# A hybrid conformer / gated-DeltaNet trunk layer on one Trainium2 core: the engine queues ordered by another scheduler simulation

## The chip, the cores and the metric

The kernel runs on one core of one Trainium2 chip, as one program with one launch. The metric is device time in microseconds (us), from three executions of each kernel; the median is what counts. A profile of one more execution gives a trace: every instruction of the five engines with its start and duration, the DMA packets and the semaphore events. TensorE (PE) does the matmuls and weight loads (PEld), VectorE (DVE) and ScalarE (ACT) do elementwise work, GpSimd (POOL) a little of it, SyncE (SP) issues nearly all the DMAs. Each engine works through a queue of its own, in the order in which the program was built; an instruction whose semaphore is not there yet holds up everything behind it on that engine.

## The reference

One layer, for 256 prompt positions and 64 sample positions together (T = 320 columns), D = 2048:

```python
h = rmsnorm(x, g_pre_mix)
p = h @ w_in                                   # 6160 columns
a_out = conformer_conv(p[..., :2048], ...)     # GLU, depthwise conv of 31 taps, group norm, silu
b_out = gdn_mixer(p[..., 2048:], ...)          # conv of 4 taps, silu, l2norm, chunked delta rule, gated norm
x = x + rmsnorm(jnp.concatenate([a_out, b_out], axis=-1) @ w_out, g_post_mix)
h = rmsnorm(x, g_pre_ffn)
gu = causal_dwconv(h @ w_up, ffn_buf, w_ffn_dw, b_ffn_dw)   # 2 x 5632 columns, 3 taps
gate, up = jnp.split(gu, 2, axis=-1)
x = x + rmsnorm((jax.nn.silu(gate) * up) @ w_down, g_post_ffn)
```

Besides both outputs, all four recurrent states are returned for both groups of positions.

## The kernel before, in words

Everything lies transposed: 128 channels on the partitions, the 320 positions along the free axis. A product of float32 accuracy is made from rounded operands: a weight tile `w` is split into `whi` (ACT, the cast of line 217) and `wlo = w - whi` (DVE, line 218), an activation likewise into `hi` and `lo`, and three matmuls of 128x128 by 320 columns replace one (weights `whi` by `hi`, `whi` by `lo`, `wlo` by `hi`; lines 233, 234 and 237 in `block_matmul`). So each 512 KB of weights costs a DMA by SP (line 210 in `load_dma`), a cast by ACT, a subtraction by DVE and 24 matmuls. The pools `wst` (raw weights) and `wsp` (split weights) have three buffers each: SP's next weight load waits for a DVE subtraction, ACT's next cast waits for matmuls.

The stages, in order:

- **Start** (lines 285 to 405): x, its scale vectors and the weights of four column blocks (`w_first`, in pairs of k: line 324) are loaded, scaled and split, and PE works through four blocks at once (`ps_first`, lines 398 and 400).
- **Input projection with both mixers** (to line 1003): 48 column blocks. The mixers' own steps are generators that are advanced between the dense matmuls. Among them are the gates (`psg`, line 479), and, for each head, squares, scales and copies on ACT (`vh`, `kd`, `kds`; lines 689 to 711).
- **Output projection** (`psm`, to line 1078): in two parts; the second (lines 1067 to 1069, five k of the sixteen) also loads x again in 16 pieces (line 1056) and two tiles of `w_up` ahead of time, all through SP's queue.
- **The middle norm** (lines 1082 to 1105): the row sums end in `rstd` (`pst`, line 259) and `rstd_rows` (`psb`, line 272), with matmuls on zeros between them (`keep_warm`, `psw`, line 280). Then, for each of the 16 k: `m[k]` times the norm (DVE, line 1099), the residual sum (DVE, line 1100), the cast to `hi2[k]` (ACT, line 1104) and `lo2[k]` (DVE, line 1105). The weights of the next stage are split in between (lines 1090 to 1095).
- **First group of the up-projection** (`up_group`, lines 1114 to 1124): four column blocks at once, so that PE can begin with k = 0 while the later k are still being made: 12 matmuls for each k, of which the first eight read `hi2[k]` and the last four `lo2[k]`.
- **ConvFFN** (to line 1207): the other 84 column blocks of `w_up`, with conv and gate on DVE and ACT, and, four times, 16 blocks of `w_down` (`psdn`). The row sums of the new x are made with `square_acc` (line 1040) and used after the first blocks (`second_norm`).
- **End**: the last norm, residual by matmul (`fin`) and the output.

The order of each queue is not written out. The program is traced in the order of the code; every instruction gets a priority (its place, shifted by `high_priority`), `issue_after` adds an order between two instructions of one engine, and the tile framework's scheduler then plays the program through in a simulation of its own, takes at each step the instruction of best priority among those it holds to be ready, and writes the queues down in the order in which it took them. The lines on which most below rests:

```python
            with ExitStack() as e:
                if 0 < k < 4:
                    e.enter_context(tc.issue_after(added))
                V.tensor_tensor(m[k], m[k], rb1, ALU.mult)
            added = V.tensor_tensor(x1[:, k, :], x1[:, k, :], m[k], ALU.add).ins
...
            S.activation(hi2[k], x1[:, k, :], AF.Identity, scale=g)
            split = V.scalar_tensor_tensor(lo2[k], x1[:, k, :], g, hi2[k].bitcast(F32), ALU.mult, ALU.subtract).ins
...
            for n, (wt, x) in enumerate(((hi, xh), (lo, xh), (hi, xl))):
                for i in range(4):
                    o = i * 256 + k % 2 * P
                    PE.matmul(pss[i][:, 0:T], wt[:, o:o + P], x, start=(k == 0 and n == 0), stop=(k == KB - 1 and n == 2))
```

## Time and profile before

| what | us |
|---|---|
| three executions | 1485.42, 1484.97, 1485.43 (median 1485.42) |
| the profiled execution | 1485.64 |
| its span, first to last instruction | 1483.9 |
| PE busy, PEld busy | 1474.3, 1452.9 |
| DVE, ACT, POOL busy | 994.5, 734.1, 234.0 |
| bytes moved by DMA | 224.22 MB, 151 GB/s on the mean |

Times in the trace count from the first instruction. A row of the timeline has start, duration, engine, line, operation and tiles; several alike in a row are merged (xcount), and the idle time of the engine before a row stands in brackets with what ended it. Matmuls overlap each other in the records: each lasts about 0.31 us, yet one starts every 0.147 us. So a wait of PE shows in the distance of two starts, and the brackets give less than the whole of it.

### The profile page before, as it was taken

What the parts mean: (1) busy time and instruction counts of PE and PEld (TensorE: products, weight loads), DVE (VectorE), ACT (ScalarE), POOL (GpSimd) and SP (SyncE); (2) the same over time, 40 slices, a digit from 0 to 9 for tenths busy, and PEclk for the clock granted to TensorE, in tenths of its full rate; (3) what the DMA queues carried; (4) which work ended last, traced back from release to release, by engine and by line L of the source; (5) the groups of instructions that cost most, each with busy time, mean ns of one, the idle gap of its engine ahead of it and who ended that gap; (6) DMA issues with size and microseconds to landing.
All of it is one profiled execution on the core that took longest, in us unless ns stands there. A gap on an engine that the chain in (4) does not pass through costs nothing.

```text
span 1483.9 us, 27312 instructions
## 1 busy us (share of the span) xinstructions
PE 1474.3 (99%) x10626; PEld 1452.9 (98%) x10626; DVE 994.5 (67%) x1812; ACT 734.1 (49%) x1355; POOL 234.0 (16%) x390
## 2 busy tenths in 40 slices
PE   9999999999999999999999999999999999999998
PEld 8999999999999989999999999999999999999997
DVE  6779888889998778765336666445666445666554
ACT  7774656665554746544334444334444334444453
POOL 0111101121010001332002222002322001223101
PEclk9999999999999999999999999999999999999999
DMA  8435453545444734444554444554444445444453
GB/s 287 148 115 157 159 162 113 151 155 147 123 126 144 243 122 142 156 143 132 147 176 144 155 148 130 146 161 164 148 150 140 137 149 173 148 156 142 137 148 119
DMA packets 98281, 224.22 MB, mean 151 GB/s; under 512 B 18792, under 2 KB 39528, under 8 KB 98152
## 3 DMA queue, kind: packets, MB, share of 16 engines
q1 hardware_dynamic: 98008, 222.45, 47.4%
q8 instruction: 83, 1.36, 0.4%
q14 instruction: 46, 0.38, 0.1%
q10 hardware_dynamic: 144, 0.03, 0.0%
HBM read 215.33 MB, written 7.12 MB: 150 GB/s over the span
## 4 chain that ended last, share of the span: by engine, by line
PE 94%; ACT 2%; DVE 1%; DMA 1%; issue 1%; POOL 0%; SPq 0%; ACTq 0%; DVEq 0%
PE psu L237 13%; PE psu L234 13%; PE psu L233 13%; PE psdn L233 7%; PE psdn L234 7%; PE psdn L237 7%; PE psq L233 3%; PE psq L234 3%; PE psq L237 3%; PE psm L233 2%; PE psm L234 2%; PE psm L237 2%; PE psu L1123 1%; PE psv L233 1%; PE psgate L233 1%; PE psgate L237 1%
## 5 line engine op out<-in xcount | busy, mean ns | idle before, releaser
L217 ACT CAST whi<-w 128x1024 fp32r<-128x1024 f32 (+2 forms) x440 | 413.1, 941 | 484.6 <-PE psu L234 169.6
L218 DVE TENSOR_TENSOR wlo<-w,whi 128x1024 fp32r<-128x1024 f32 (+2 forms) x440 | 477.1, 1085 | 194.6 <-ACT whi L217 126.6
L234 PE MATMUL psu<-lo,whi 128*128 128x320 f32 x1344 | 397.0, 309 | 0.0
L233 PE MATMUL psu<-hi,whi 128*128 128x320 f32 x1344 | 396.9, 309 | 0.0
L234 PEld LDWEIGHTS psu<-lo,whi 128*128 128x128 f32 x1344 | 252.3, 188 | 0.0
L233 PEld LDWEIGHTS psu<-hi,whi 128*128 128x128 f32 x1344 | 252.3, 188 | 0.0
L237 PE MATMUL psu<-hi,wlo 128*128 128x320 f32 x1344 | 224.3, 309 | 0.0
L237 PEld LDWEIGHTS psu<-hi,wlo 128*128 128x128 f32 x1344 | 204.0, 188 | 0.0
L234 PE MATMUL psdn<-gl,whi 128*128 128x320 f32 x660 | 195.9, 310 | 0.0
L1156 POOL COPY nffn<-fbuf 128x2 f32<-128x2 f32 x88 | 101.6, 1155 | 587.2 <-DVE fbuf L1154 584.0
L1154 DVE TENSOR_TENSOR fbuf<-psu,rb 128x256 f32<-128x256 f32 x88 | 37.4, 424 | 168.7 <-PE psu L237 168.7
L233 PE MATMUL psdn<-gh,whi 128*128 128x320 f32 x480 | 142.8, 309 | 0.0
L234 PEld LDWEIGHTS psdn<-gl,whi 128*128 128x128 f32 x660 | 123.9, 188 | 0.3
L233 PE MATMUL psq<-hh,whi 128*128 128x320 f32 x352 | 105.9, 314 | 0.0
L234 PE MATMUL psq<-hl,whi 128*128 128x320 f32 x352 | 104.1, 309 | 0.0
L233 PEld LDWEIGHTS psdn<-gh,whi 128*128 128x128 f32 x480 | 90.1, 188 | 0.0
L237 PE MATMUL psdn<-gh,wlo 128*128 128x320 f32 x480 | 89.8, 309 | 0.0
L237 PEld LDWEIGHTS psdn<-gh,wlo 128*128 128x128 f32 x480 | 75.3, 188 | 0.0
L233 PEld LDWEIGHTS psq<-hh,whi 128*128 128x128 f32 x352 | 66.1, 188 | 0.5 <-issue 0.2
L234 PEld LDWEIGHTS psq<-hl,whi 128*128 128x128 f32 x352 | 66.1, 188 | 0.2
L563 DVE SCALAR_TENSOR_TENSOR cvt<-ub,par,cvt 128x320 f32<-128x320 f32 x120 | 65.2, 544 | 0.1
L1199 DVE TENSOR_TENSOR y<-y,psdn 128x320 f32<-128x320 f32 x45 | 22.0, 488 | 59.1 <-PE psdn L237 59.1
(356 smaller groups left out, 2477.1 us busy)
## 6 DMA issues: line engine op xcount, KB each, us to landing
w<-in_w_up SPq DMA_DIRECT2D x176, 512.0 KB
w<-in_w_in SPq DMA_DIRECT2D x88, 512.0 KB
w<-in_w_down SPq DMA_DIRECT2D x64, 384.0 KB
w<-in_w_down SPq DMA_DIRECT2D x64, 320.0 KB
w<-in_w_out SPq DMA_DIRECT2D x32, 320.0 KB
w<-in_w_out SPq DMA_DIRECT2D x16, 384.0 KB
w<-in_w_first SPq DMA_DIRECT2D x6, 512.0 KB
wtp<-wsp SPq DMA_DIRECT2D x4, 640.0 KB
```

Of the source, the lines that this page charges most:

```text
L217: S.copy(hi[:, 0:width], w[:, 0:width])
L218: V.tensor_tensor(lo[:, 0:width], w[:, 0:width], hi[:, 0:width].bitcast(F32), ALU.subtract)
L233: tick(PE.matmul(ps, wh, xh, start=(first and k0 + j == 0), stop=False))
L234: tick(PE.matmul(ps, wh, xl, start=False, stop=False))
L237: tick(PE.matmul(ps, lo[:, j * P:(j + 1) * P], xh, start=False, stop=(final and k0 + j == nk - 1)))
L563: return lambda: V.scalar_tensor_tensor(acc, x, w, acc, ALU.mult, ALU.add)
L1123: PE.matmul(pss[i][:, 0:T], wt[:, o:o + P], x, start=(k == 0 and n == 0), stop=(k == KB - 1 and n == 2))
L1154: V.tensor_tensor(buf[:, 2:258], psu[:, 0:TP], rb2[:, 0:TP], ALU.mult)
L1156: G.tensor_copy(nffn[:, b, 0, :], buf[:, 256:258])
L1199: V.tensor_tensor(y[:, n, :], y[:, n, :], psd[:, 0:T], ALU.add)
```

## The change

The tile framework has a second simulation that its scheduler can play the program through. It follows the engines and transfers more finely than the default. One argument selects it:

```diff
-    with tile.TileContext(nc) as tc:
+    with tile.TileContext(nc, schedule_with_timeline_sim=True) as tc:
         trunk_kernel(tc, ins, outs)
```

No operation, tile, buffer or priority changes; what changes is the order in each engine's queue, and with it the places of some waits. (Two loads of activation tables on ACT fall away, since functions of one table now stand together more often.) PE's order is nearly the old one; the mixers' small matmuls stand some matmuls earlier or later among the dense ones. Three places where DVE, SP and ACT differ:

DVE in the middle norm, before. Here `m` with a number is `m[k]`: 5575, 5658, 5714 and 5766 are k = 2, 3, 4 and 5, `psb` is the norm's row, `lo_0` to `lo_3` are `lo2[0]` to `lo2[3]`, and `wlo` is a split of the weights for the first group:

```order
L1105 SCALAR_TENSOR_TENSOR lo_0_6880<-x_6336,par,hi_0_6879 128x320
L218 TENSOR_TENSOR wlo<-w,whi 128x1024
L1105 SCALAR_TENSOR_TENSOR lo_1_6892<-x_6336,par,hi_1_6891 128x320
L1100 TENSOR_TENSOR x_6336<-x_6336,m_5575 128x320
L1099 TENSOR_TENSOR m_5658<-m_5658,psb 128x320
L1099 TENSOR_TENSOR m_5714<-m_5714,psb 128x320
L1105 SCALAR_TENSOR_TENSOR lo_2_6898<-x_6336,par,hi_2_6897 128x320
L1100 TENSOR_TENSOR x_6336<-x_6336,m_5658 128x320
L218 TENSOR_TENSOR wlo<-w,whi 128x1024
L1105 SCALAR_TENSOR_TENSOR lo_3_6910<-x_6336,par,hi_3_6909 128x320
L1100 TENSOR_TENSOR x_6336<-x_6336,m_5714 128x320
L1099 TENSOR_TENSOR m_5766<-m_5766,psb 128x320
```

The same place now; 6842 is k = 15, and the marks stand for one more multiplication and `lo_1`, with nine multiplications behind it, and for ten sums:

```order
L1105 SCALAR_TENSOR_TENSOR lo_0_6880<-x_6336,par,hi_0_6879 128x320
L218 TENSOR_TENSOR wlo<-w,whi 128x1024
L1100 TENSOR_TENSOR x_6336<-x_6336,m_5575 128x320
L1099 TENSOR_TENSOR m_5658<-m_5658,psb 128x320
L1099 TENSOR_TENSOR m_5714<-m_5714,psb 128x320
...
L1099 TENSOR_TENSOR m_6842<-m_6842,psb 128x320
L1105 SCALAR_TENSOR_TENSOR lo_2_6898<-x_6336,par,hi_2_6897 128x320
L1100 TENSOR_TENSOR x_6336<-x_6336,m_5658 128x320
L218 TENSOR_TENSOR wlo<-w,whi 128x1024
L1100 TENSOR_TENSOR x_6336<-x_6336,m_5714 128x320
...
L1100 TENSOR_TENSOR x_6336<-x_6336,m_6842 128x320
L1105 SCALAR_TENSOR_TENSOR lo_3_6910<-x_6336,par,hi_3_6909 128x320
```

Before, DVE went k by k; now all multiplications (line 1099) stand ahead of `lo_2`, and all sums (line 1100) ahead of `lo_3`. Ahead of `lo_1` stand one sum and three multiplications more than before, between `lo_1` and `lo_2` ten multiplications (k = 6 to 15), between `lo_2` and `lo_3` thirteen sums and one split.

SP in the second part of the output projection, before; `w<-in_w_out` is a weight load of that part, `x` a piece of x, `w<-in_w_up` a tile for the first group of the up-projection:

```order
L210 DMA w<-in_w_up 128x4x256
L1056 DMA x_6336<-in_x 128x320 x5
L210 DMA w<-in_w_out 128x640
L1056 DMA x_6336<-in_x 128x320 x2
L210 DMA w<-in_w_out 128x640 x2
L1056 DMA x_6336<-in_x 128x320
```

And now:

```order
L210 DMA w<-in_w_up 128x4x256
L1056 DMA x_6336<-in_x 128x320 x8
L210 DMA w<-in_w_out 128x640
L1056 DMA x_6336<-in_x 128x320
L210 DMA w<-in_w_out 128x640
```

Three pieces of x more stand ahead of the first weight load; further on, one piece of x and `fpar` (line 1058) now follow the second `w_up` tile at once, where a weight load stood.

ACT among the steps of a head in the input projection, before; `whi` is a cast of dense weights, the other rows are the head's own scales (`vh`, `kds`) and silu (`kq`):

```order
L710 ACTIVATE kds_599<-tv_1296,sc 64x128
L711 ACTIVATE vh<-tv_1296,sc 128x128
L636 ACTIVATE kq<-cq 128x256
L637 ACTIVATE kqs<-cq 128x64
L217 CAST whi<-w 128x1024 x3
```

And now:

```order
L694 ACTIVATE tq_1312<-ssq_597,eps 128x3
L217 CAST whi<-w 128x1024
L625 COPY qb_594<-par 128x3
L711 ACTIVATE vh<-tv,sc 128x128 x2
L706 ACTIVATE kd<-tkq,sc 128x128 x2
L710 ACTIVATE kds_599<-tv_1296,sc 64x128 x2
L711 ACTIVATE vh<-tv_1296,sc 128x128
L636 ACTIVATE kq<-cq 128x256
L637 ACTIVATE kqs<-cq 128x64
L217 CAST whi<-w 128x1024
```

The three casts that stood together behind the whole head's work are now spread through it.

Two smaller moves are spoken of below. At the start, SP now issues the last two loads of x (four k), the constants `cst` and `wba` and `cst2` ahead of the last three `w_first` loads. And on PE, at each first block of `w_down`, the last k's matmuls (`gp`, `gl`) now stand behind nearly all of the second block's first half, where before they stood in its middle; likewise `psg` and the second norm's `pst` have moved by a few tens of dense matmuls or less.

## The prediction

> **What bounds the kernel now.** I read the page first, for who is busy and whose work the chain that ended last consists of; then windows, for the stretches in which PE is not full; then the timeline of those stretches, row by row. From the page:
>
> ```profile
> PE 1474.3 (99%) x10626; PEld 1452.9 (98%) x10626; DVE 994.5 (67%) x1812; ACT 734.1 (49%) x1355; POOL 234.0 (16%) x390
> ...
> PE 94%; ACT 2%; DVE 1%; DMA 1%; issue 1%; POOL 0%; SPq 0%; ACTq 0%; DVEq 0%
> ```
>
> PE is busy for 1474.3 of 1483.9 us, and 94% of the chain is PE. So a new order of the queues can win a few us at most, while whatever makes PE wait is lost in full. The windows (window, its length, then busy time and count of each engine, clock, DMA share, GB/s) say where DVE is near its limit too:
>
> ```profile
> core 0: us, PE busy (x) PEld busy (x) DVE busy (x) ACT busy (x) POOL busy (x), PEclk, DMA share, GB/s
> 10.00:20.00 10.00, 10.00 (x70) 9.88 (x69) 8.84 (x13) 9.47 (x16) 0.00 (x0) 1.00 0.92 348
> 540.00:560.00 20.00, 19.71 (x129) 18.68 (x129) 19.54 (x39) 10.29 (x16) 0.00 (x0) 1.00 0.39 133
> 600.00:700.00 100.00, 100.00 (x682) 99.72 (x681) 63.53 (x113) 45.56 (x61) 28.34 (x44) 1.00 0.45 142
> ```
>
> In the ConvFFN (600 to 700) PE is full and DVE has a third of its time free: a moved DVE instruction is hidden there. From 540 to 560, the middle norm beside the first group of the up-projection, DVE is busy for 19.54 of 20 us and PE still for 19.71: DVE only just delivers what PE eats next. In such a place order is everything, and it is where the change moves DVE most.
>
> **The first group of the up-projection: the main term.** DVE there before (start, duration, engine, line, operation, tiles, count in a row):
>
> ```profile
> 535.86 1.22 DVE L218 TENSOR_TENSOR wlo<-w,whi 128x1024 fp32r<-128x1024 f32 x1
> 537.00 0.54 DVE L1105 SCALAR_TENSOR_TENSOR lo<-x,par,hi 128x320 fp32r<-128x320 f32 x1
> 537.46 0.48 DVE L1100 TENSOR_TENSOR x<-x,m 128x320 f32<-128x320 f32 x1
> 537.86 0.88 DVE L1099 TENSOR_TENSOR m<-m,psb 128x320 f32<-128x320 f32 x2
> 538.66 0.55 DVE L1105 SCALAR_TENSOR_TENSOR lo<-x,par,hi 128x320 fp32r<-128x320 f32 x1
> ```
>
> Distances of starts are the price of one in a full queue: a multiplication (line 1099) (538.66 − 537.86)/2 = 0.40, a sum (line 1100) 537.86 − 537.46 = 0.40, a `lo` (line 1105) 537.46 − 537.00 = 0.46 with its result there after 0.55, a split 537.00 − 535.86 = 1.14. PE at the same time, and at the group's end:
>
> ```profile
> 534.92 1.11 PE L1123 MATMUL psu<-hi,whi 128*128 128x320 f32 x4
> ...
> 537.04 0.75 PE L1123 MATMUL psu<-hi,whi 128*128 128x320 f32 x4
> ...
> 538.22 0.75 PE L1123 MATMUL psu<-lo,whi 128*128 128x320 f32 x4
> 538.80 0.75 PE L1123 MATMUL psu<-hi,whi 128*128 128x320 f32 x4
> ...
> 549.94 0.85 PE L1123 MATMUL psu<-hi,whi 128*128 128x320 f32 x4
> ...
> 564.33 0.75 PE L1123 MATMUL psu<-lo,whi 128*128 128x320 f32 x4
> ```
>
> One k costs PE 538.80 − 537.04 = 1.76 (12 at 0.147), of which the `lo` part, its last four, begins 1.18 after the first and lasts 0.59. A restart after a wait costs 0.10 (0.85 against 0.75). The group starts at 534.92 and ends at 564.33 + 4 × 0.147 = 564.9. Now I put the new row of DVE on this clock, from the split on, which both orders have at 535.86 with the same work ahead of it:
>
> - 537.00 the sum of k = 2, 537.40 three multiplications, 538.60 `lo2[1]`, there at 539.15. PE wants it at 538.22: **0.9 lost**.
> - 539.06 ten multiplications (4.0), 543.06 `lo2[2]`, there at 543.61. PE, 0.9 and a restart late, has done k = 1 at 539.85 and wants it 1.18 later, at 541.0: **2.6 lost**.
> - 543.52 the sum of k = 3, there at 544.0; ACT's cast to `hi2[3]` (some 0.57) brings 544.6, when PE, done with k = 2 at 544.3, waits: **0.3 lost**. Then 543.92 a split, 545.06 twelve sums (4.8), 549.86 `lo2[3]`, there at 550.4. PE wants it at 544.6 + 0.1 + 1.18 = 545.9: **4.5 lost**.
> - The `lo` part and a restart end at 551.1; twelve k at 1.76 end at 572.2.
>
> The wait's cover being gone, nothing else stands on PE's queue behind k = 3 but k = 4. After that nothing of this is late: the remaining `lo` come every 0.46, PE takes 1.76 for each. Next late would be a weight split: the buffer for that of k = 10 comes free when PE ends k = 5 at 551.1 + 2 × 1.76 = 554.6; ACT's cast (some 1.05), the split (1.22) and five `lo` ahead of it (2.3) give 559.2, and PE wants k = 10 at 551.1 + 6 × 1.76 = 561.7. So the group ends 572.2 − 564.9 = **7.3 us later**. Without the four restarts (0.4) and the wait for `hi2[3]` (0.3), which no row shows in this form, it is 6.6.
>
> **What the change gives and takes elsewhere.** Waits of PE in other stages, and the rows that stand behind them:
>
> ```profile
> 69.25 0.40 PE L479 MATMUL psg<-gt,cst 128*128 128x16 f32 x2 [0.20 <-DVE gt L462]
> ...
> 110.88 0.42 PE L233 MATMUL psz<-hh,whi 128*128 128x320 f32 x1 [0.58 <-ACT whi L217]
> ...
> 509.00 0.41 PE L1069 MATMUL psm<-bh,wlo 128*128 128x320 f32 x1 [1.05 <-DVE wlo L218]
> ...
> 577.63 0.83 PE L259 MATMUL pst<-cst,acc 128*128 128x1 f32 x6 [0.23 <-DVE acc L1040]
> ...
> 697.38 0.31 PE L233 MATMUL psdn<-gh,whi 128*128 128x320 f32 x1
> 697.62 0.41 PE L233 MATMUL psdn<-gp,whi 128*128 128x320 f32 x1
> ```
>
> A record lasts 0.31 and the next may start after 0.147, so a bracket understates the wait by 0.16. `psg` loses 0.36, the second norm's `pst` 0.39, and each now stands where its input has more time: −0.4 each. At 110.88 PE waits 0.74 for a cast, because three of them stand together behind a head's scales:
>
> ```profile
> 109.79 2.93 ACT L217 CAST whi<-w 128x1024 fp32r<-128x1024 f32 x3
> ```
>
> Spread out, they come in time: −0.8 with the restart. At each first block of `w_down` PE steps through the last k haltingly (697.38 to 697.62 is 0.24 where 0.147 is due, 0.09 lost; there are three such steps, 0.28); behind the second block's half their input has long been there: four times, −1.1. Credits: −2.7; a wait that only changes its place makes them 0.
>
> SP in the second part of the output projection:
>
> ```profile
> 489.38 2.23 SPq L1056 DMA_DIRECT2D x<-in_x  x5
> ```
>
> A piece of x takes SP 2.23/5 = 0.45 to issue. Three more ahead of the first weight load put it 1.3 later, one more piece and `fpar` ahead of a later load put that 0.9 later. This part has no cover: PE lost 1.2 for a split at 509.00 already. Both delays landing in full are +2.2; if the three buffers ahead soak them up and the wait at 509.00 goes, since x is then out of the way, −1.2. I take +1.0, above their middle (+0.5), because these loads are the late thing already.
>
> At the start, four x loads of two k in all (640 KB), the constants and `cst2` (about 580 KB by their shapes) go ahead of three `w_first` loads. The first of the three (k = 10 and 11) feeds the cast of the first row here, and the second row shows PE at the last matmuls of k = 8 and 9:
>
> ```profile
> 19.47 1.05 ACT L351 CAST whi<-w 128x1024 fp32r<-128x1024 f32 x1
> ...
> 22.43 1.34 PE L398 MATMUL ps_first<-hh,wlo 128*128 128x320 f32 x8
> ```
>
> 1220 KB at the 348 GB/s of 10 to 20 are 3.5 us: the cast would end at 19.47 + 1.05 + 3.5 = 24.1, and PE wants it at 22.43 + 8 × 0.147 = 23.6: +0.5 (0 if the transfers overlap otherwise, +1.0 if the rate falls to 300).
>
> ConvFFN's many small moves on DVE, POOL and ACT I cost at nothing: the free third of DVE at 600 to 700 hides them, and were it gone, PE's share of 100.00 there would fall.
>
> **The sum**, on the profiled execution of 1485.64 (span 1483.9, 1.7 around it): +7.3 + 1.0 + 0.5 − 0.8 − 0.4 − 0.4 − 1.1 = +6.1, so 1491.7. The median of the three runs is 0.22 below the profiled one: **1491.5**.
>
> **The rivals.** First, the clock. PE's clock is not full at once:
>
> ```profile
> 1.42 3.55 PE L280 MATMUL psw<-wz 128*128 128x512 bf16 x8 [1.42 <-POOL wz L250]
> ...
> 532.95 2.32 PE L280 MATMUL psw<-wz 128*128 128x512 bf16 x10
> ```
>
> After its idle start a `psw` matmul takes 0.44 (3.55/8), later 0.23. No wait in the trace of before is over 1.4 us, and the granted clock is 1.00 around all of them; in the changed kernel there is one of 4.5. If it brings the half pace back for as long as at the start, 3.5 us of PE's work lose half: +1.75, **1493.2**. [...]
>
> Second, transfers: the later weight loads bite in full and every credit is only a wait moved: 7.3 + 2.2 + 1.0 = +10.5, **1495.9**. Against it: `psg` and `pst` read one small tile each, so more distance must help.
>
> Third, next to nothing: group, weight loads and start at their lower ends, with all credits: 6.6 − 1.2 + 0 − 2.7 = +2.7, **1488.1**. That is within 0.2% of the median (2.97 us, about what a measurement of this kernel can tell from no change). All ends at once are needed, or that I misplaced one of the two batches.
>
> Fourth, faster: PE's waits of today vanish (2.7 of credits and 1.2 at 509.00), and the group costs nothing, 1485.4 − 3.9 = **1481.5**. It decides if `lo2[3]` is there before about 541.7, when PE would want it (538.80 + 1.76 + 1.18). But the new row has from 537.00 fourteen sums, thirteen multiplications and three more instructions ahead of it on one engine, 12.9 us. It could hold only if DVE were three times as quick.
>
> **How the numbers follow.** The forecast 0.50, the clock 0.28, transfers 0.06, next to nothing 0.12, faster 0.04. The range takes in the first three and stops short of the last two: from the forecast with group and start at their low ends and the weight loads at −0.6 (1491.5 − 0.7 − 0.5 − 1.6 = 1488.7, put at 1488.3 for the small moves that I cost at nothing) to the transfers' 1495.9. Slower by over 0.2%: 0.50 + 0.28 + 0.06 = 0.84; within: 0.12; faster: 0.04.
>
> **What would show it.** In the profile of the changed kernel: on DVE a row of line 1099 with a count of about ten and one of line 1100 with about twelve, where before the counts are one and two; on PE, line 1123, three waits of about 0.9, 2.6 and 4.5 us, each before `lo,whi`, the releaser a DVE `lo`; the group from first to last about 37 us instead of 30. After the 4.5 us, rows of four that take 0.75 say the clock stayed, rows of 1.3 that it fell. At the first `w_down` blocks no step of 0.24; no bracket at `psg`, at the second norm's `pst` and at the first `psz`. The prediction is wrong if the group still lasts about 30 us, or if its loss is there and the total isn't: then what I cost at nothing carries the difference.

## The result and the profile after

The changed kernel takes 1499.99 us (median of four executions, 1498.32 to 1501.31) where the kernel before takes 1485.33 beside it (1484.97 to 1485.43): 1.0096 times as long, with an interval of 1.0083 to 1.0108. That is 14.7 us slower, far above the range. The profiled execution took 1498.73, its span is 1496.9. The line of its page with the busy times, and the shares of the chain that ended last:

```profile
PE 1478.4 (99%) x10625; PEld 1458.3 (97%) x10626; DVE 994.8 (66%) x1812; ACT 731.0 (49%) x1353; POOL 236.3 (16%) x390
...
PE 91%; DVE 3%; DMA 2%; ACT 1%; issue 1%; POOL 0%; SPq 0%; ACTq 0%; DVEq 0%
```

The busy times are the old ones, so no work was added. The chain has more of DVE (3% for 1%) and of DMA (2% for 1%): PE waits more. Where, the starts of PE's rows tell. I cut both timelines at the same instructions: the last `ps_first`, the first and the last matmul of lines 1067 to 1069, the first and the last of line 1123, the first `fin`. In e1, e7, e12 and e16 below, 15 to 21 matmuls of the next blocks stand among those of line 1123; they are counted to the ConvFFN.

| part of the program | before, us | changed, us | difference | foreseen |
|---|---|---|---|---|
| start | 34.0 | 35.1 | +1.1 | +0.5 |
| input projection with the mixers, output projection, first part | 453.1 | 452.1 | −1.0 | −1.2 |
| output projection, second part | 42.6 | 47.0 | +4.4 | +1.0 |
| middle norm up to the group | 5.2 | 5.2 | 0 | 0 |
| first group of the up-projection | 29.8 | 39.4 | +9.6 | +7.3 |
| ConvFFN | 905.1 | 903.7 | −1.4 | −1.5 |
| end | 14.0 | 14.4 | +0.4 | 0 |
| sum | 1483.8 | 1496.9 | +13.1 | +6.1 |

The same windows as before. From 540 to 560 PE has fallen from 19.71 to 12.71, DVE is busy throughout, and the granted clock is 0.74:

```profile
10.00:20.00 10.00, 10.00 (x70) 10.00 (x69) 7.20 (x12) 7.61 (x13) 0.00 (x0) 1.00 0.96 358
540.00:560.00 20.00, 12.71 (x62) 11.52 (x61) 20.00 (x44) 7.95 (x18) 0.00 (x0) 0.74 0.26 79
600.00:700.00 100.00, 100.00 (x684) 100.00 (x683) 68.47 (x128) 47.98 (x64) 32.81 (x51) 1.00 0.46 148
```

DVE in the group of the changed kernel; the two batches are the rows with a count of 10 and 12:

```profile
541.92 1.27 DVE L1099 TENSOR_TENSOR m<-m,psb 128x320 f32<-128x320 f32 x3
543.12 0.54 DVE L1105 SCALAR_TENSOR_TENSOR lo<-x,par,hi 128x320 fp32r<-128x320 f32 x1
543.58 4.06 DVE L1099 TENSOR_TENSOR m<-m,psb 128x320 f32<-128x320 f32 x10
547.56 0.54 DVE L1105 SCALAR_TENSOR_TENSOR lo<-x,par,hi 128x320 fp32r<-128x320 f32 x1
...
549.56 4.90 DVE L1100 TENSOR_TENSOR x<-x,m 128x320 f32<-128x320 f32 x12
554.38 0.54 DVE L1105 SCALAR_TENSOR_TENSOR lo<-x,par,hi 128x320 fp32r<-128x320 f32 x1
```

And PE beside it:

```profile
543.71 0.85 PE L1123 MATMUL psu<-lo,whi 128*128 128x320 f32 x4 [0.99 <-DVE lo L1105]
...
548.15 0.86 PE L1123 MATMUL psu<-lo,whi 128*128 128x320 f32 x4 [2.42 <-DVE lo L1105]
549.15 1.02 PE L1123 MATMUL psu<-hi,whi 128*128 128x320 f32 x4
549.97 1.27 PE L1123 MATMUL psu<-hi,wlo 128*128 128x320 f32 x4
554.98 1.44 PE L1123 MATMUL psu<-lo,whi 128*128 128x320 f32 x4 [3.74 <-DVE lo L1105]
556.21 1.27 PE L1123 MATMUL psu<-hi,whi 128*128 128x320 f32 x4
...
561.41 0.75 PE L1123 MATMUL psu<-hi,whi 128*128 128x320 f32 x4
```

The three waits stand where they were foreseen, each ended by a `lo`: with the 0.16 that a bracket leaves out 1.15, 2.58 and 3.90 (foreseen 0.9, 2.6, 4.5). The small wait for `hi2[3]` is there too: from 548.15 to 549.15 are 1.00 where four matmuls and a restart need 0.69, so 0.3 as foreseen. Besides, rows of four take 1.27 instead of 0.75, and that begins at 549.7, behind the second wait and ahead of the third: PE runs at half pace. 21 matmuls start 0.267 apart instead of 0.147, 2.5 us in all. The third wait came out shorter than 4.5 because the half pace ahead of it made PE late: with full pace ahead (e9 below) it is 4.55.

The second part of the output projection: PE's longest wait, SP's new queue, and ACT's casts (a bracket names what ended the wait):

```profile
511.29 0.42 PE L1067 MATMUL psm<-bh,whi 128*128 128x320 f32 x1 [1.82 <-ACT whi L217]
512.15 0.64 PE L1069 MATMUL psm<-bh,wlo 128*128 128x320 f32 x1 [0.30 <-DVE wlo L218]
```

```profile
490.35 3.65 SPq L1056 DMA_DIRECT2D x<-in_x  x8
...
503.47 0.38 SPq L1058 DMA_DIRECT2D fpar<-in_fpar  x1
504.15 17.93 SPq L210 DMA_DIRECT2D w<-in_w_out  x9
```

```profile
507.65 1.05 ACT L217 CAST whi<-w 128x1024 fp32r<-128x1024 f32 x1 [1.32 <-DMA w<-in_w_up]
...
510.51 0.72 ACT L217 CAST whi<-w 128x640 fp32r<-128x640 f32 x1 [0.85 <-DMA w<-in_w_out]
```

The wait for a split at 509.00 has gone and a longer one for a cast has come; ACT in its turn waited for two loads. Behind it, too, eleven matmuls start 0.267 apart. At the start it is the cast of k = 10 and 11 that waits for its load, and PE for the cast:

```profile
23.48 1.04 ACT L351 CAST whi<-w 128x1024 fp32r<-128x1024 f32 x1 [0.66 <-DMA w<-in_w_first]
```

```profile
24.58 0.42 PE L398 MATMUL ps_first<-hh,whi 128*128 128x320 f32 x1 [0.83 <-ACT whi L351]
```

The credits came as foreseen: `psg`, the second norm's `pst` and the first `psz` have no bracket any more, and at each first block of `w_down` the halting steps are gone (the distance to before shrinks by 0.27 there, four times).

The second part scatters between executions: in the seven profiles of kernels that keep the changed order there (the changed kernel twice, e1, e5, e6, e8, e9) it took 44.7 to 47.7 us.

### The profile page after: what moved, and what is told of

It is laid out like the page before. It is cut to its first block, busy times and chain, and to the rows that moved or that the text cites. A ratio compares the mean times of both kernels' runs of the same rounds, so it can differ in the third digit from the quotient of the medians.

```text
span 1496.9 us, 27322 instructions
## 1 busy us (share of the span) xinstructions
PE 1478.4 (99%) x10625; PEld 1458.3 (97%) x10626; DVE 994.8 (66%) x1812; ACT 731.0 (49%) x1353; POOL 236.3 (16%) x390
## 4 chain that ended last, share of the span: by engine, by line
PE 91%; DVE 3%; DMA 2%; ACT 1%; issue 1%; POOL 0%; SPq 0%; ACTq 0%; DVEq 0%
PE psu L233 13%; PE psu L234 13%; PE psu L237 13%; PE psdn L233 6%; PE psdn L234 6%; PE psdn L237 6%; PE psq L233 3%; PE psq L237 3%; PE psq L234 3%; PE psm L233 2%; PE psm L234 2%; PE psm L237 2%; PE psu L1123 2%; PE psv L237 1%; PE psv L233 1%; PE psv L234 1%
## 5 line engine op out<-in xcount | busy, mean ns | idle before, releaser
L563 DVE SCALAR_TENSOR_TENSOR odd<-ub,par,odd 128x320 f32<-128x320 f32 x112 | 60.8, 543 | 0.2
```

The costliest lines, as they stand in the source:

```text
L563: return lambda: V.scalar_tensor_tensor(acc, x, w, acc, ALU.mult, ALU.add)
```

## The experiments

The theory after the result: three places cost, each by its order alone (the start's loads, the weight loads of the output projection's second part, DVE's norm in batches), and PE's half pace follows the waits. (A total is given beside the median of the kernel before on the same chip.) The rivals: the loss is in one place and the others follow from it; the transfers or the clock were disturbed anyway.

**The norm's order.** e1 puts DVE back to k by k in the changed kernel:

```diff
-                if 0 < k < 4:
-                    e.enter_context(tc.issue_after(added))
+                if 0 < k:
+                    e.enter_context(tc.issue_after(added if k < 4 else los[k - 3]))
...
-    with tc.high_priority(offset=60):
+    with tc.high_priority(offset=60), tc.issue_after(los[-1]):
         for k in range(KB):
             square_acc(k, x1[:, k, :], True)
```

> The changed kernel, with DVE's queue in the middle norm put back to k by k (products, sums and lo of one k together, the sums of squares behind the last lo); SP, POOL and PE keep the changed order. Theory (DVE's two batches make PE wait, and the waits bring the slow pace): the group of line 1123 goes from 39.7 us back to about 30, the total from 1498.3-1501.3 to about 1489-1491. Rival (the group is slow because the transfers or the clock were already disturbed when it began): the group stays above 35 us and the total above 1495.

The group took 29.4 us, no matmul of it at half pace. The total was 1493.07 (1490.22 to 1495.17) beside 1487.55 for before on that chip, 5.5 us more where the changed kernel lost 14.7. The kernel before scatters too, and on this chip lay high: five of its eleven executions here are near 1485.6 and six near 1487.8, so losses beside 1487.55 (e1, e2, e4, e5) may be some 2 us too small. The group's loss is DVE's order. The total lay higher than expected, and the profiled execution (1495.17, the highest of six) shows one reason, a start that ended at 39.5, not 35.1:

```profile
25.14 1.04 ACT L351 CAST whi<-w 128x1024 fp32r<-128x1024 f32 x1 [3.10 <-DMA w<-in_w_first]
```

```profile
26.24 0.64 PE L398 MATMUL ps_first<-hh,whi 128*128 128x320 f32 x1 [3.24 <-ACT whi L351]
26.67 0.47 PE L400 MATMUL ps_first<-hl,whi 128*128 128x320 f32 x1
```

The same wait as at 24.58 in the changed kernel, but 3.24 long, with half pace behind it (0.47 for one). So the start's cost scatters from one execution to the next.

e4 does the reverse: the kernel before, its norm written out in the changed order.

```diff
+        def behind(fn, *args):
+            with ExitStack() as e:
+                if queued[0] is not None:
+                    e.enter_context(tc.issue_after(queued[0]))
+                queued[0] = fn(*args).ins
...
+        rest(1)
+        for k in range(6, KB):
+            product(k)
+        rest(2)
+        total(3)
+        weights(3)
+        for k in range(4, KB):
+            total(k)
+        for k in range(3, KB):
+            rest(k)
```

> The kernel before, with DVE's queue in the middle norm written out in the changed kernel's order (all products ahead of lo of k = 2, all sums ahead of lo of k = 3); all else before's. Theory: this alone makes the group 7.3 us longer by waits and about 2.3 by the slow pace: total 1492.6 if the pace stays full, about 1495 if it falls. Rival (the order of DVE alone is harmless): within 2 us of before.

1494.32 (1492.64 to 1495.14) beside 1487.55; in its profile the group took 39.5 us, and every other part was that of before within 0.6 us (span 1493.3 against 1483.9). The order of DVE's queue alone costs the 9.6 us (9.66 in this profile).

**The half pace.** e5 gives PE matmuls on zeros to do in the three waits; e8 only in the third, e9 only in the first two (`fill` is `{3: 17}` and `{1: 4, 2: 10}`):

```diff
+        pss += [ps_t.tile([P, 512], F32, tag="t", name="psu") for _ in range(2)]; psw2, mm, fill = ps_g.tile([P, 512], F32, tag="g", name="psw2"), None, {1: 4, 2: 10, 3: 17}
...
+                own = keep_warm(psw2, fill[k], mm) if n == 2 and k in fill else None
```

> The changed kernel, with 4, 10 and 17 matmuls on zeros (0.23 us each) put on PE's queue ahead of the lo part of k = 1, 2 and 3, so that PE works through the three waits. Theory (the slow pace follows from the waits): no row of line 1123 is slower than 0.85 per four, the group takes about 37.3 instead of 39.7 us, total some 2.3 us below the changed kernel. Rival (the slow pace has nothing to do with idle time): rows of four at 1.27 stay, and the total is the same or a little above.

```profile
549.08 3.84 PE L280 MATMUL psw<-wz 128*128 128x512 bf16 x17
553.62 0.85 PE L1123 MATMUL psu<-lo,whi 128*128 128x320 f32 x4 [0.70 <-DVE lo L1105]
554.31 0.74 PE L1123 MATMUL psu<-hi,whi 128*128 128x320 f32 x4
```

The matmuls on zeros end 0.7 before `lo` comes, so the wait itself has its full length; behind it rows take 0.74, and the group 37.20 us instead of 39.43. So the waits cost 37.20 − 29.85 = 7.35, and the half pace the other 2.2. (Total 1497.46 beside 1487.55.)

> The changed kernel, with 17 matmuls on zeros before the lo part of k = 3 only, so that PE stays idle in the waits of about 0.9 and 2.6 us and has work in the third. Theory (waits of 2 to 3 us are enough for the slow pace): the matmuls on zeros and hi rows of k = 3 run slow behind the second wait (0.44 each, or 1.27 per four) in this run. [...]

```profile
548.81 1.39 PE L1123 MATMUL psu<-lo,whi 128*128 128x320 f32 x4 [2.40 <-DVE lo L1105]
549.99 1.27 PE L1123 MATMUL psu<-hi,whi 128*128 128x320 f32 x4
551.06 1.27 PE L1123 MATMUL psu<-hi,wlo 128*128 128x320 f32 x4
552.13 3.93 PE L280 MATMUL psw<-wz 128*128 128x512 bf16 x17
```

No wait of the group is longer than 2.6 us, and the half pace comes all the same, for some 3.3 us (the three rows from 548.81 to 552.13); behind it a `psw` takes 0.23 again. (1497.11 beside 1485.64.)

> The changed kernel, with 4 and 10 matmuls on zeros before the lo parts of k = 1 and 2, so that only the third wait, of about 4 us, is left idle. Theory: that wait alone also brings the slow pace: rows of four at 1.27 behind it for some 3.4 us, group about 39 us. Rival (it needs the waits one after another): rows of 0.75 behind it, group about 37.3.

The third wait alone, 4.4 us and the bracket's 0.16, brings it as well:

```profile
549.41 0.74 PE L1123 MATMUL psu<-hi,wlo 128*128 128x320 f32 x4
554.55 1.44 PE L1123 MATMUL psu<-lo,whi 128*128 128x320 f32 x4 [4.39 <-DVE lo L1105]
555.78 1.27 PE L1123 MATMUL psu<-hi,whi 128*128 128x320 f32 x4
```

The next two rows take 1.27 too. Total 1498.97 beside 1485.64. Either wait does it, 2.56 us in e8 and 4.55 in e9.

**The weight loads of the output projection's second part.** e2, in the changed kernel, and e10, in the kernel before, issue each piece of x behind the weight load of its own block:

```diff
-        hi, lo = load_split(ins["w_out2"][n], nk2 * P)
+        (hi, lo), own = load_split(ins["w_out2"][n], nk2 * P), sent[0]
...
-        nc.sync.dma_start(x1[:, n:n + 1, :], ins["x"][:, n:n + 1, :])
+        with tc.issue_after(own): nc.sync.dma_start(x1[:, n:n + 1, :], ins["x"][:, n:n + 1, :])
```

> The changed kernel, with each piece of x in the output projection's second part issued behind the weight load of its own block (and fpar behind the last); nothing else is forced. Theory (pieces of x ahead of weight loads on SP's queue are what that part loses): the wait of 2 us before 511 and the slow matmuls behind it go, PE ends the part 3 to 4.5 us earlier, total about 1494-1497. Rival (the transfers are full there whatever the order, so the wait only moves): the part still loses over 3 us and the total stays within 1 us of the changed kernel.

The part took 43.25 us instead of 47.0 (44.7 at the least in the changed order), no matmul of it at half pace; total 1497.41 (1493.84 to 1498.40) beside 1487.55.

e13 is the reverse, the kernel before with the changed order of x (block n's weights behind these pieces; `fpar` with the last):

```diff
+    ahead = {5: (0, 8), 6: (8, 9), 7: (9, 11), 8: (11, 14), 9: (14, 16)}
```

> The kernel before, with the changed kernel's order on SP in the output projection's second part alone (eight pieces of x ahead of the next weight load, then 1, 2, 3 and 2 with fpar). Theory (this order alone is the part's loss): the part takes 46 to 47 us instead of 42.6, with a wait of about 2 us for a cast and slow matmuls behind it, total some 4 us above the kernel before. Rival (the loss needs the changed order of the other engines too): part below 44 us, total within 1.5 us.

```profile
509.18 0.42 PE L1072 MATMUL psm<-bh,whi 128*128 128x320 f32 x1 [1.54 <-ACT whi L217]
```

(Here line 1072 is what was 1067.) The part took 45.7 us, twelve matmuls at half pace; total 1488.11 (1486.85 to 1490.78) beside 1485.63. SP's order alone costs 2.5 (by the medians) to 3.1 (by the part) of the 4.4 us; where the rest comes from, the other engines' order or the scatter of this part, no run shows.

> The kernel before, with each piece of x in the output projection's second part issued behind the weight load of its own block. Theory (pieces of x ahead of weight loads cost that part time in before as well, 1.9 us of its 42.6): the wait of 1.2 us at 509 shrinks, total 0 to 1.5 us below the kernel before. Rival (the part is bound by its bytes whatever the order): total within 0.3 us.

A miss: 1485.83 beside 1485.63, ratio 1.000 (0.9991 to 1.0009). The profiled execution, the slowest of eleven (1486.84), shows that the waits only move: that of 1.05 at 509 (brackets) has shrunk to 0.51 and 0.30, two new ones of 0.70 and 0.61 stand at 522 and 525, and the part took 44.1 us. This move of x wins nothing in the order of before.

**The start.** e6 puts the changed kernel's loads back in turn, e11 gives before the changed order:

```diff
-                    load_x(*kk)
-                    load_first(*kk)
-            nc.sync.dma_start(cst, ins["cst"][:, 0:NCST1])
+                    with (tc.issue_after(fed[-1]) if fed else ExitStack()): load_x(*kk)
+                    fed.append(load_first(*kk).ins)
+            with tc.issue_after(fed[-1]): nc.sync.dma_start(cst, ins["cst"][:, 0:NCST1])
```

> The changed kernel, with the loads of the start put back on SP: x and w_first in turn, the constants cst and wba behind the last w_first (cst2 may stay ahead). Theory (the start loses 1 us in good executions and 3 to 4 in others, as the casts of the last three w_first wait for transfers that now stand ahead of them, and PE, idle for 2 us or more, also comes back at half pace): PE ends the start near 34 us as before, not at 35 to 39.5; the spread of the executions shrinks, and the median falls by 1 to 3 us against the changed kernel. Rival (the start's spread is the chip's own and comes with either order): PE's end of the start stays at 35 or later, total unchanged.

The start ended at 34.5; 1498.04 (1495.82 to 1498.84) beside 1485.64, 12.4 us above before where the changed kernel was 14.7 above. The spread stayed at 3 us, so in that point the rival holds. (On SP `par`, `gpar` and `cst2` still stand farther ahead than before.)

```diff
+            for part in "x0 f0 x1 f1 x2 f2 x3 f3 X4 F4 X6 F6 X8 X10 X12 F8 X14 c F10 F12 F14".split():
```

> The kernel before, with the changed kernel's order of the start's loads alone: the last x loads and the constants cst and wba ahead of the last three w_first (cst2 stays behind). Theory (this order makes PE wait, 1 us in the best executions and, with the slow pace, up to 5): PE ends the start at 35 to 39 us instead of 34.0, total 1 to 4 us above the kernel before, with a wide spread. Rival (the chip's own scatter made the start differ, not the order): PE ends near 34 us or in the spread that before shows, total within 0.5 us.

The start ended at 34.65 in the profiled execution, which was the fastest of eleven; these run from 1486.37 to 1490.27 with a median of 1487.71, beside 1485.63: ratio 1.0014 (1.0005 to 1.0022). The order costs 2.1 us in the middle and up to 4.6.

**All three.** e14 is the kernel before with e4, e11 and e13 at once; e15 is the changed kernel on the same chip.

> The kernel before, with all three orders of the changed kernel written out at once: the start's loads as in e11, x ahead of the weight loads as in e13, DVE's norm in batches as in e4. Theory (these three are the change's whole cost, and they add up): the parts take about 35 to 37 (start's end), 46 and 39.6 us, total 1498 to 1500, at or a little above the changed kernel on the same chip, since the changed kernel's gains elsewhere (about 2 us) are missing. Rival (the cost lies partly elsewhere, or the losses overlap when together): total below 1496.

> The changed kernel itself, beside the others on the same chip. Theory (its scatter of 3 us comes from the start, where PE's wait for the cast of k = 10 has another length in each execution): 1497.5 to 1501.5, the profile's start at 35 to 39 us and the other parts within 0.5 us of the first profile's (452.1, 47.0, 39.4, 903.7). Rival (the scatter comes from the waits in the group or the clock): the start near 35.1 and other parts different.

e14: 1498.54 (1497.69 to 1499.49); e15: 1499.70 (1497.97 to 1499.94); before 1485.59. Ratios 1.0085 (1.0071 to 1.0099) and 1.009 (1.0076 to 1.0104): the three orders alone make the kernel before as slow as the changed one, within the intervals. By parts they agree less well: in e14's profile the start ended at 34.2 (it was expected at 35 to 37), the second part took 46.0 and the group 39.7; in e15's the start ended at 35.5, the second part took 47.7, the group 39.8, and the rest was as in the first profile within 0.3. So in e14 the start and the second part lose some 3 us less than in e15, and the changed kernel's gains in the projections and the ConvFFN, some 2.5 us, are missing. Over all profiled executions with the changed start (the changed kernel twice, e1, e2, e5, e8, e9) it ended between 35.1 and 39.5, on the mean at 36.8, 2.8 later than before; in e11 and e14, which have the order of the loads alone, at 34.65 and 34.2.

**Mending all three.** e7 joins e1, e2 and e6.

> The changed kernel with all three put back: DVE's middle norm by k, x behind its block's weight load, the start's loads in turn. Theory (these three places are all that the change costs, and elsewhere it gains some 1.5 us): about 1 us below the kernel before, to the same. Rival (the loss is spread over more places, or one of them takes over when another is mended): 2 us or more above the kernel before.

1487.11 (1485.36 to 1488.22) beside 1485.64, ratio 1.0005 (0.9996 to 1.0014). The group took 29.4 and the second part 42.4, but the start ended at 37.5, and a new wait (1.81 in brackets) came at the second norm's `psb`, which now stands right behind `pst`. The start's edit is that of e6, where it ended at 34.5: x and `w_first` in turn do not mend the start by themselves. e12 puts `par`, `gpar` and `cst2` behind as before, too, and the sums from `lo` of k = 11 on (the edit of the sums):

```diff
-            square_acc(k, x1[:, k, :], True)
+            with tc.issue_after(los[min(k + 10, KB - 1)]): square_acc(k, x1[:, k, :], True)
```

> The changed kernel with all three places put back more closely: the start's loads wholly as before (par, gpar and cst2 too), x behind its block's weight load, DVE's middle norm by k with the sums of squares from lo of k = 11 on. Theory (the rest of the changed order gains some 1.5 us, and the e7 run gave 2 us of it back at psb of the second norm, where the sums of squares came late): start near 34.0, no wait at that psb, 1 to 2.5 us below the kernel before. Rival (the start scatters by itself, and mending one place moves the wait to the next): total at or above the kernel before.

```profile
577.31 0.72 PE L259 MATMUL pst<-cst,acc 128*128 128x1 f32 x6
579.84 0.66 PE L272 MATMUL psb<-cst,rr 128*128 128x128 f32 x3 [1.81 <-POOL rr L265]
```

1486.42 (1484.35 to 1487.83) beside 1485.63, no gain: the start ended at 33.7, but `psb` stood right behind `pst` on PE and waited 1.81, with half pace behind it. e16 changes one number, after how many dense matmuls the norm goes on:

```diff
-        yield 12, 1, 0
+        yield 24, 1, 0
```

> The e12 version, with psb of the second norm some 30 matmuls behind its pst instead of directly behind it. Theory (e12 lost 1.8 us and then the slow pace, some 3.4 us in all, at that psb): no bracket at psb, the part from the group to the last norm back near 903.7 to 904.5 us, total 1482.0 to 1484.0, 1.5 to 3 us below the kernel before. Rival (the next wait takes its place): that part stays above 906 us and the total within 0.5 us of the kernel before.

```profile
578.21 0.72 PE L259 MATMUL pst<-cst,acc 128*128 128x1 f32 x6
583.57 0.49 PE L272 MATMUL psb<-cst,rr 128*128 128x128 f32 x3
```

1482.46 (1482.05 to 1483.87) beside 1485.59: ratio 0.9978 (0.9968 to 0.9987). With the three places mended, and `psb` moved, the new order beats both kernels, by 3.1 us the one before. Its parts: start 34.0, projections 452.0, second part 43.4, group 29.4, ConvFFN 903.7, end 14.4.

## Why the prediction was wrong

The direction and the largest term were right, the size was not: +6.1 foreseen, +13.1 in the profiled execution.

- **The group, +7.3.** Right, as a sum and in its pieces: e5, where the pace stays full, has 7.35, and the waits are 1.15, 2.58, 0.3 and, with full pace ahead (e9), 4.55 (foreseen 0.9, 2.6, 0.3, 4.5).
- **The pace.** The step that failed is the one that kept the pace full in the forecast because "No wait in the trace of before is over 1.4 us": that said nothing of what a longer one brings. The loss was set down as a rival with +1.75 and 0.28, and only behind the 4.5 us wait. The pace fell in the groups of the changed kernel, e4 and e9, where waits of 2.6 or 4.5 us were left idle (rows of 1.27; in the changed kernel +2.2 to 2.5), in e8 behind the 2.6 alone, and also in the second part of the output projection (eleven matmuls, 1.3 us) and at the start of e1 and e7 (matmuls of 0.47).
- **The second part, +1.0 with +2.2 as the upper end; measured +4.4.** The failed step counted too few transfers: three more pieces of x ahead of the first weight load and one more with `fpar` ahead of a later one. SP's rows of both kernels show more ahead of each of the five loads that follow the first `w_up`: 8, 9, 11, 14 and 16 pieces, the last with `fpar`, where 5, 7, 7, 8 and 10 stood. The fifth is the load of the cast at 510.51. Six pieces and `fpar` at the prediction's own 0.45 are 3.1 us, and some 3 us came through as waits and 1.3 as half pace. Their bytes, six times 160 KB and 264 KB, are 5.2 us at the 240 GB/s of 500 to 520 in the changed kernel (an estimate), so either price explains the wait, and no run separates them. That bytes have a part is likely: this load took 6.3 us from issue to landing, the same loads issued at 486.14 and 513.66 took 2.9 and 3.1.
- **The start, +0.5 up to +1.0; measured +1.1 in the first profile and 2.8 on the mean.** The mechanism was right (the cast of k = 10 is late), the size was that of one rate; the load's arrival scatters (its cast at 23.48 or, in e1, at 25.14), and behind e1's wait of 3.24 in brackets came half pace too.
- **The credits, −2.7; measured −2.4 before the +0.4 at the end**, which was not foreseen. There PE does eight `fin` of x behind `psb` where it did six, and the first `fin` of y starts 0.5 later; no experiment tests that.
- **The transfers' rival** (+10.5) came nearest in number, by luck: it denied the credits, which came, and knew nothing of the half pace. Only its weight loads in full were right.

Of the 7.0 us between +6.1 and +13.1 the half pace is 3.6 (2.3 and 1.3), the second part's waits 2.1, the start 0.6, credits and end 0.7. The median lies another 1.3 above the profiled execution.

What stays open: why the load of k = 10 and 11 arrives 1.7 us later in one execution (the cast at 25.14, e1) than in another (23.48).

## What to carry to other kernels

When instructions are only reordered, read each in-order queue for batches: work that is ready early and needed late must not stand ahead of work that PE wants next. For a moved transfer, count at every load that is waited for what now stands ahead of it, in issues and in bytes, not only at the first. And reckon with more than the wait itself: here the half pace cost 1.3 us behind a wait of 2.0 (the second part) and 2.2 to 2.5 behind those of 2.6 and 3.9 (the group), and matmuls on zeros in the waits kept the pace (e5, a group of 37.20 us beside 39.43).

## What the runs showed of the hardware

Waits of PE shorter than I had thought brought half pace: single ones of 2.0 (511.29, the changed kernel), 2.1 (e7's start) and 2.6 us (e8). The granted clock shows the half pace too. In the changed kernel:

```profile
510.00:515.00 5.00, 3.41 (x13) 3.15 (x14) 4.34 (x8) 3.84 (x7) 0.37 (x3) 0.71 0.48 143
545.00:550.00 5.00, 2.44 (x15) 1.92 (x14) 5.00 (x12) 0.56 (x1) 0.00 (x0) 0.97 0.00 0
550.00:555.00 5.00, 1.26 (x6) 0.86 (x5) 5.00 (x14) 4.93 (x11) 0.00 (x0) 0.50 0.36 105
555.00:560.00 5.00, 5.00 (x19) 5.00 (x20) 5.00 (x10) 0.97 (x3) 0.00 (x0) 0.51 0.34 106
560.00:565.00 5.00, 5.00 (x36) 5.00 (x35) 4.82 (x10) 2.14 (x4) 0.00 (x0) 1.00 0.01 2
```

In the group the clock reads 0.50 and 0.51 from 550 to 560, the third wait included (the first row of 1.27 starts at 549.97, the next of 0.75 at 560.24); in the second part the rows are slow from 512.15 to 515.51. The length of the bracket alone does not tell whether it comes. At the second norm's `psb` PE waited 1.81 in brackets in e12 and in e7: behind it matmuls started 0.267 apart in e12 (580.56 to 583.23) and 0.147 in e7 (from 583.71 on). What decided there, no run shows. At the start, where the prediction speaks of a clock that is not full, a `psw` took 0.44 in the kernel before; the granted clock reads 1.00 from 1.40 to 4.90, so the rows alone show that pace.
